# The end of a chunk in an output projection: stores in pieces, sums a row at a time, a gain vector loaded in quarters

## The chip, the cores and the metric

The kernel runs on one core of a Trainium2 chip. A core has five engines, each with an instruction stream of its own that it takes strictly in order: TensorE (PE; products and, listed apart as PEld, the loads of its weights), VectorE (DVE), ScalarE (ACT), GpSimd (POOL) and SyncE (SP). Transfers between HBM and the on-chip memory SBUF are issued by an engine's queue (SPq, ACTq, POOLq) and carried out by 16 shared DMA engines. Products go to PSUM, from where VectorE and ScalarE read them.

The metric is the device time of one execution, in microseconds; the median of several runs counts.

## The reference

One inference step of a one-layer encoder with two groups of heads, for 1024 prompt rows and 128 sample rows (8 streams of 16), all in float32. What matters here is its end:

```python
y = jnp.concatenate([y_sb, y_r], axis=-1)          # 2048 wide, from both groups of heads
out = jnp.einsum('bte,ed->btd', y, w_out)          # w_out: 2048 x 2048
x = x + rms_norm(out, norm_post)                   # rms over the 2048 columns of a row
```

So each of the 1152 rows of `out` needs its mean square over all 2048 columns before any of its columns can be finished: `x + out * norm_post / sqrt(mean(out^2) + eps)`.

## The kernel before

Rows are handled in tiles of 128: eight of the prompt (0 to 7) and SAMPLE. The input projection, both attentions and the retention fill the first 1980 us or so; they leave the concatenated heads, transposed, in HBM (`s_y`). The output projection then takes nine row tiles in three chunks of three: chunk 1 is (0, 1, 2), chunk 2 is (4, 5) and (6), chunk 3 is (3, SAMPLE) and (7).

**Panels.** A chunk is computed in panels of 512 columns (`out_panel`, L1010). For each of 16 blocks `k` of 128 inner rows, a 128 x 512 block of `w_out` is loaded by SP (L1018) and split into a high and a low half (`split`, L128): ScalarE writes the high half rounded to fp32r (L129), VectorE the rest (L130). Then each of the three row tiles takes three products (high x high, L1028; high x low weights, L1029; low x high, L1030), which add up in the row tile's own PSUM bank. The buffers `wr`, `wh` and `wl` of a block exist four times, so the splits can run some blocks ahead of the products. Panels use two PSUM pools by turns.

**Sums.** When a panel is through, `take` (L1074) is called for each row tile: ScalarE squares the bank and sums the squares along the row into one column of `ssq` (L1076), VectorE multiplies the bank by `norm_post` into the row's `out` buffer (L1077). `norm_post` lies in `gpost`, the same 2048 values on all 128 partitions, loaded by one transfer on ScalarE's queue (L1045). That buffer, like `rp` and the second PSUM pool, is opened only when the stage of the attentions has closed (L1040). Chunk 1's first panel is computed within that stage, among its last jobs (L1036).

**Finish.** After the fourth panel, `scales` (L1079) turns the four sums of squares into 1/rms (L137 to L143), and `store` (L1084) finishes the rows in halves of 1024 columns. For the first and second row tile VectorE scales and adds `x` in one instruction (L1090); for the third ScalarE scales (L1087) and GpSimd adds `x` (L1088). The transfer to HBM is issued from ScalarE's queue (L1091), behind its sum. The chunk's `x` rows were loaded in its third and fourth panels (`load_x_rows`, each tied behind a load of `w_out` in SP's queue, L1020). There are five `out` buffers for rows, three for `x` rows and two for `ssq`.

**Chunk 3** is different: its last panel is 256 columns wide, and the other 256 columns' weights are kept split in SBUF (`keep_last`), so that the rows end one after the other, each with its own scales and four pieces of 512 columns, stored from SP's queue (L1108 to L1120).

**Jobs and ticks.** Side work is written as generators. `Job(steps, after)` puts one into a list; `tick()` (L173), called once after each row tile's three products, advances a clock and runs the next step of at most one job that is due; a step's `yield` says how many ticks later the next one is due. `fetch` (L1004) loads and splits the next chunk's rows that way, a step every 6 ticks, during the first two panels of a chunk. `drain` ticks until a job is done.

The order in which the program writes instructions is a priority: a planner lays the streams out by its own estimate of when each instruction's inputs are there, so an instruction can stand ahead of others that were written before it. On the chip the streams are then taken in that order, and an engine waits for the inputs of its next instruction.

Of the kernel before, what the change touches and what calls it, by code (L numbers as in the profile page):

```python
# [16 lines left out]
P = 128  # L17
D = 2048
# [30 lines left out]
D_TI = (32, 13)  # L49
D_OUT = 4  # L50
D_KL = 29
D_MR = 6
EPS = 1e-6
SCALE = 1.0 / math.sqrt(P)
# [4 lines left out]
def tile_hybrid_step(  # L59
# [26 lines left out]
    nc = tc.nc  # L86
# [86 lines left out]
    def tick():  # L173
        clock[0] += 1
        for job in jobs:
            if job.at <= clock[0]:
                wait = step(job)
                jobs.remove(job)
                if wait is None:
                    job.done = True  # L180
                else:
                    job.at = clock[0] + wait
                    jobs.append(job)
                return

    def drain(job):
        while job is not None and not job.done:
            tick()
# [4 lines left out]
    def moving(pool, n):  # L193
        return [list(x) for x in zip(*(moving_part(pool, n, q) for q in range(KT // WQ)))]

    def load_moving(mov, at, n, src, stage=None):
        hi, lo = mov
        for k in range(KT):
# [7 lines left out]
            split(hi[q][:, j, at : at + n], lo[q][:, j, at : at + n], r)  # L206
            yield D_MR

# [91 lines left out]
    with ExitStack() as s1:  # L300
# [47 lines left out]
        with tc.tile_pool(name="p0", bufs=2) as p0, tc.tile_pool(name="p0s", bufs=1) as p0s, tc.tile_pool(  # L348
# [50 lines left out]
            scales = [stats(0)]  # L399
            for i, t in enumerate(tiles):  # L400
# [6 lines left out]
                if i == 1:  # L407
                    w4 = list(load_w(col(4, 0)))
                    loaded += [load_x(t) for t in tiles[3:]]
                    acc = acc_banks(g0)  # L410
# [482 lines left out]
        for gi, g in enumerate(GROUPS):  # L893
            tiles, n, nt = g["tiles"], g["n"], len(g["tiles"])
# [141 lines left out]
        panel0 = out_panel(chunk1, 0, (accp,), D_OUT, loads)  # L1036
# [3 lines left out]
    with ExitStack() as s3:  # L1040
        c3 = s3.enter_context(tc.tile_pool(name="c3", bufs=1))
        rp = s3.enter_context(tc.tile_pool(name="rp", bufs=1))
        accq = s3.enter_context(tc.tile_pool(name="accq", bufs=2, space=PSUM))
        gpost = c3.tile([P, D], F32, name="gpost")
        nc.scalar.dma_start(gpost, norm_post[0].partition_broadcast(P))  # L1045

        LAST = slice(7 * 256, 8 * 256)

        def keep_last(at):

            hi, lo = main
            for q in range(KT // WQ):
                for j in range(0, WQ, 2):
                    wr = wp.tile([P, 2, 256], F32, name="wr4", tag="wr")
                    k = (q * WQ + j) * P
                    nc.sync.dma_start(wr, w_out[0, k : k + 2 * P, LAST].rearrange("(k p) e -> p k e", p=P))
                    split(hi[q][:, j : j + 2, at : at + 256], lo[q][:, j : j + 2, at : at + 256], wr)
                    yield D_KL

        def out_project(chunk, panel0=None, kept=None):  # L1060
            m = len(chunk)
            parts = 4 if kept is None else 5
            outs = [rp.tile([P, D], F32, name="out", tag="out", bufs=5) for _ in chunk]
            ssq = rp.tile([P, m, 5], F32, name="ssq3", tag="ssq3", bufs=2)
            xrs = []

            def load_x_rows():
                for t, _, _, _ in chunk:
                    xr = rp.tile([P, D], F32, name="xr", tag="xr", bufs=3)
                    nc.sync.dma_start(xr, x_rows(t))  # L1070
                    xrs.append(xr)
                    yield

            def take(n, a, c, cols):  # L1074
                sq = rp.tile([P, 512], F32, name="sq3", tag="sq3", bufs=1)
                nc.scalar.activation(sq[:, : a.shape[1]], a, AF.Square, accum_out=ssq[:, n, c : c + 1])  # L1076
                nc.vector.tensor_tensor(outs[n][:, cols], a, gpost[:, cols], ALU.mult)  # L1077

            def scales(n0, n1):  # L1079
                tot = rp.tile([P, n1 - n0], F32, name="tot", tag="tot", bufs=2)  # L1080
                nc.vector.tensor_reduce(tot, ssq[:, n0:n1, :parts], mybir.AxisListType.X, ALU.add)
                return inv_rms(rp, tot, D, f"out{n1 - n0}")

            def store(n, rs, cols, pool, q=nc.scalar):  # L1084
                o = outs[n][:, cols]
                if pool:
                    nc.scalar.activation(o, o, AF.Copy, scale=rs)  # L1087
                    nc.gpsimd.tensor_tensor(o, o, xrs[n][:, cols], ALU.add)  # L1088
                else:
                    nc.vector.scalar_tensor_tensor(o, o, rs, xrs[n][:, cols], ALU.mult, ALU.add)  # L1090
                q.dma_start(y_rows(chunk[n][0])[:, cols], o)  # L1091

            rows = load_x_rows()
            for p in range(4):
                width = 512 if kept is None or p < 3 else 256
                acc = panel0
                if p or not panel0:
                    acc = out_panel(chunk, p, (accp, accq), 1, None, rows if p >= 2 else None, width)
                for n in range(m):
                    take(n, acc[n][:, :width], p, slice(p * 512, p * 512 + width))  # L1100
            if kept is None:
                rs = scales(0, m)
                for half in range(2):
                    for n in range(m):
                        store(n, rs[:, n : n + 1], slice(half * D // 2, (half + 1) * D // 2), n == m - 1)
                return
            drain(job)
            for n, (_, _, (hi, lo), at) in enumerate(chunk):  # L1108
                a = accp.tile([P, 512], F32, name="a4", tag=f"acc{n % 2}")[:, :256]
                ts = slice(at, at + P)  # L1110
                for k in range(KT):
                    q, j = divmod(k, WQ)
                    wh, wl = (main[c][q][:, j, kept : kept + 256] for c in range(2))
                    nc.tensor.matmul(a, hi[q][:, j, ts], wh, start=(k == 0), stop=False)
                    nc.tensor.matmul(a, hi[q][:, j, ts], wl, start=False, stop=False)
                    nc.tensor.matmul(a, lo[q][:, j, ts], wh, start=False, stop=(k == KT - 1))
                take(n, a, 4, LAST)
                rs = scales(n, n + 1)
                for c in (3, 0, 1, 2):
                    store(n, rs, slice(c * 512, (c + 1) * 512), c == 3, nc.sync)  # L1120

        side = moving(c3, P)
        chunk2 = part(1, (4, 5), main, 3 * P), part(1, (6,), side, 0)
        chunk3 = part(0, (3, SAMPLE), main, 0), part(1, (7,), main, 2 * P)
        ready = [Job(fetch(c), 4) for c in chunk2]
        out_project(chunk1, panel0)
        for job in ready:
            drain(job)
        ready = [Job(fetch(c), 4) for c in chunk3]
        out_project(chunk2[0] + chunk2[1])  # L1130
        for job in ready:
            drain(job)
        keep = 3 * P
        job = Job(keep_last(keep), D_KL)
        out_project(chunk3[0] + chunk3[1], kept=keep)


# [70 lines left out]
```

## Time and profile before

| | |
|---|---|
| runs | 2405.13, 2405.88, 2412.4 us |
| median | 2405.88 us |
| profiled execution, first to last instruction (the page has no other time of it) | 2398.4 us |
| TensorE busy | 2331.4 us, 97% |
| VectorE, ScalarE, GpSimd busy | 52%, 38%, 27% |
| mean granted TensorE clock | 0.994 |
| products of the output projection's panels (L1028 to L1030) | first at 1981.7 us, last started at about 2371 us |

How to read the rows: in a timeline, start in us, duration in us, engine (with q: its queue), line, operation, what is written `<-` what is read, partitions x elements, count, and in brackets how long the engine had been idle before and what ended that. Several like instructions in a row are merged into one with their count. In groups: count, busy time, mean ns of one, idle time before. In windows: stretch, length, then busy time and count of each engine named, granted clock, share of the DMA engines, GB/s.

### The profile page before, as it was taken

Reading aid. Unit: us, or ns where it says so; the run is one execution under the profiler, and the core shown is the slowest. Engines: PE = TensorE matmul, PEld = TensorE weight load, DVE = VectorE, ACT = ScalarE, POOL = GpSimd, SP = SyncE. Lnnn points to the kernel's source line nnn. Section 1 sums busy time; section 2 is a strip of 40 time slices with the busy share of each in tenths; the row PEclk is TensorE's granted clock in tenths of the full one; section 3 lists DMA queues with packets and bytes.
Section 4 is the critical chain, followed back from the end, with each engine's and each line's share of the span. In section 5 each row is a group of like instructions: output and inputs, shape, how many; then the busy total and the mean of one; then the engine's idle time right before and its main releaser. Section 6 shows DMA issues by size and latency. Waiting matters only on the chain.

```text
span 2398.4 us, 40493 instructions
## 1 busy us (share of the span) xinstructions
PE 2331.4 (97%) x14832; PEld 2093.7 (87%) x14832; DVE 1257.5 (52%) x2434; ACT 919.6 (38%) x1933; POOL 643.0 (27%) x1029
## 2 busy tenths in 40 slices
PE   7999999999999999998999999999999999999998
PEld 7998899999999999988878889889898887878787
DVE  7245545445554555445545554554554665564544
ACT  6323333333333333324433434343343454543343
POOL 3144353444344353443202112020221230000000
PEclk9999999999999999999999999999999999999999
DMA  7658879797889879798975565565565666765554
GB/s 244 164 131 209 162 169 196 169 203 166 184 179 194 184 167 194 176 198 198 200 191 151 139 157 149 133 157 146 142 160 139 157 177 181 231 207 176 191 182 132
DMA packets 674890, 418.68 MB, mean 175 GB/s; under 512 B 224513, under 2 KB 619777, under 8 KB 672257
## 3 DMA queue, kind: packets, MB, share of 16 engines
q1 hardware_dynamic: 524272, 285.99, 47.8%
q0 software_dynamic: 32256, 71.36, 13.6%
q10 hardware_dynamic: 118160, 58.74, 9.1%
q8 instruction: 116, 1.90, 0.4%
q14 instruction: 86, 0.70, 0.1%
HBM read 336.24 MB, written 79.69 MB: 173 GB/s over the span
## 4 chain that ended last, share of the span: by engine, by line
PE 87%; DVE 4%; DMA 4%; issue 2%; ACT 1%; POOL 1%; ACTq 0%; DVEq 0%; SPq 0%; POOLq 0%
PE acc L227 45%; PE accn L286 17%; PE a L1029 5%; PE a L1030 5%; PE a L1028 5%; PE pa L616 3%; PE z L586 2%; DMA wr<-w_in 1%; PE zc L659 1%; PE pd L726 1%; DMA mr<-s_h 1%; DVE wl L130 1%; PE pa L770 1%; DVE out L1090 1%; PE rs L752 1%
## 5 line engine op out<-in xcount | busy, mean ns | idle before, releaser
L227 PE MATMUL acc<-mh,wh 128*128 128x256 f32 (+2 forms) x2304 | 664.3, 341 | 6.4 <-ACT wh L129 6.0
L227 PE MATMUL acc<-ml,wh 128*128 128x384 f32 (+2 forms) x2304 | 663.0, 340 | 0.0
L130 DVE TENSOR_TENSOR wl<-wr,wh 128x512 fp32r<-128x512 f32 (+1 forms) x576 | 392.7, 688 | 515.5 <-ACT wh L129 508.3
L227 PE MATMUL acc<-mh,wl 128*128 128x256 f32 (+2 forms) x2304 | 658.9, 339 | 0.6 <-DVE wl L130 0.5
L129 ACT ACTIVATE wh<-wr 128x512 fp32r<-128x512 f32 (+1 forms) x576 | 356.9, 624 | 713.1 <-PE acc L227 243.4
L227 PEld LDWEIGHTS acc<-mh,wh 128*128 128x128 f32 x2304 | 420.2, 189 | 43.3 <-ACT wh L129 7.1
L227 PEld LDWEIGHTS acc<-mh,wl 128*128 128x128 f32 x2304 | 424.4, 189 | 31.4 <-issue 2.1
L227 PEld LDWEIGHTS acc<-ml,wh 128*128 128x128 f32 x2304 | 422.6, 189 | 33.2 <-issue 5.3
L643 POOL DMA_DIRECT2D kc<-cache_sb_k x512 | 332.4, 655 | 369.8 <-DVE kcT L681 207.5
L286 PE MATMUL accn<-whn,mh 128*128 128x256 f32 x1152 | 329.0, 287 | 0.9 <-ACT whn L129 0.8
L286 PE MATMUL accn<-wln,mh 128*128 128x256 f32 x1152 | 326.2, 283 | 0.7 <-DVE wln L130 0.7
L286 PE MATMUL accn<-whn,ml 128*128 128x256 f32 x1152 | 326.0, 283 | 0.0
L286 PEld LDWEIGHTS accn<-whn,mh 128*128 128x128 f32 x1152 | 220.5, 192 | 10.8 <-issue 6.7
L1029 PE MATMUL a<-wl,mh 128*128 128x512 f32 (+1 forms) x576 | 219.7, 381 | 7.8 <-DVE wl L130 7.8
L286 PEld LDWEIGHTS accn<-wln,mh 128*128 128x128 f32 x1152 | 221.2, 192 | 1.7 <-DVE wln L130 0.9
L286 PEld LDWEIGHTS accn<-whn,ml 128*128 128x128 f32 x1152 | 221.2, 192 | 0.0
L1030 PE MATMUL a<-wh,ml 128*128 128x512 f32 (+1 forms) x576 | 218.9, 380 | 0.0
L1028 PE MATMUL a<-wh,mh 128*128 128x512 f32 (+1 forms) x576 | 218.0, 380 | 0.0
L130 DVE TENSOR_TENSOR wln<-wrn,whn 128x512 fp32r<-128x512 f32 x128 | 87.5, 687 | 119.2 <-ACT whn L129 118.5
L129 ACT ACTIVATE whn<-wrn 128x512 fp32r<-128x512 f32 x128 | 80.1, 633 | 152.2 <-PE accn L286 69.8
L1029 PEld LDWEIGHTS a<-wl,mh 128*128 128x128 f32 x576 | 108.3, 188 | 30.5 <-DVE wl L130 9.9
L479 POOL DMA_DIRECT2D be<-s_be x128 | 94.2, 742 | 132.7 <-DMA s_be<-be 114.7
(189 smaller groups left out, 2604.8 us busy)
## 6 DMA issues: line engine op xcount, KB each, us to landing
wr<-w_in SPq DMA_DIRECT2D x384, 256.0 KB, 4.2
wr<-w_out SPq DMA_DIRECT2D x184, 256.0 KB, 3.6
wrn<-w_in SPq DMA_DIRECT2D x128, 256.0 KB, 3.1
kc<-cache_sb_k POOLq DMA_DIRECT2D x512, 64.0 KB, 4.5
vc<-cache_sb_v SPq DMA_DIRECT2D x64, 512.0 KB, 8.6
xt<-x_prompt SPq DMA_DIRECT2D x8, 1024.0 KB, 5.6
xr<-x_prompt SPq DMA_DIRECT2D x8, 1024.0 KB, 6.2
out<-out ACTq DMA_DIRECT2D x12, 512.0 KB, 2.9
```

The costliest lines, as they stand in the source:

```text
L129: nc.scalar.activation(hi, src, AF.Copy)
L130: nc.vector.tensor_tensor(lo, src, hi.bitcast(F32), ALU.subtract)
L227: last = nc.tensor.matmul(a[:, :m], lhs[:, j, :], rhs[w][:, j, o : o + m], start=(w == 0 and j == 0 and n == 0), stop=(w == KT // WQ - 1 a ...
L286: anchor[0] = nc.tensor.matmul(a, lhs[q][:, jj, ts], rhs[:, j, :], start=(w == 0 and j == 0 and n == 0 and t % 2 == 0), stop=(w == KT // 2 ...
L479: q.dma_start(raw[32 * i : 32 * i + 32, :].rearrange("p (k a) -> p k a", a=32), s[:, :, 32 * i : 32 * i + 32].rearrange("k (j b) a -> b (k ...
L586: nc.tensor.matmul(z[:, :c], q2[a][:, i * P : (i + 1) * P], k2[b][:, s : s + c], start=(m == 0), stop=(m == 2),)
L616: nc.tensor.matmul(po[:, :P], at[:, j, :], vn[:, j, :], start=(j == 0), stop=(j == t))
L643: nc.gpsimd.dma_start(kc[32 * i : 32 * i + 32, :].rearrange("p (k d) -> p k d", d=32), cache_k[0, 2 * c + j, s * 512 : (s + 1) * 512, h, 3 ...
L659: mm = nc.tensor.matmul(z[r, :], qp[:, j, r], ready[2 * j + c // 2][:, c % 2, :], start=(j == 0), stop=(j == 1),)
L1028: nc.tensor.matmul(a[:, :width], hi[q][:, j, ts], wh, start=(k == 0), stop=False)
L1029: nc.tensor.matmul(a[:, :width], hi[q][:, j, ts], wl, start=False, stop=False)
L1030: nc.tensor.matmul(a[:, :width], lo[q][:, j, ts], wh, start=False, stop=(k == KT - 1))
```

## The change

`norm_post` is loaded by four transfers of 512 columns instead of one of 2048. In chunks 1 and 2 the panel sums become jobs: the three calls of `take` come 4 ticks after the panel (12 for chunk 1's first) and 4 ticks apart, within the next panel. The fourth panel's job goes on, also a step every 4 ticks, with the scales and then twelve stores of 512 columns instead of six of 1024: four column pieces by three row tiles. It runs along the products of the next chunk. Chunk 3 takes its sums as before, and drains the earlier chunks' jobs after its panels.

```diff
+D_TK = 4
+D_FIN = 4
...
-        nc.scalar.dma_start(gpost, norm_post[0].partition_broadcast(P))
+        for c in range(4):
+            nc.scalar.dma_start(
+                gpost[:, c * 512 : (c + 1) * 512], norm_post[0, c * 512 : (c + 1) * 512].partition_broadcast(P)
+            )
...
-                for n in range(m):
-                    take(n, acc[n][:, :width], p, slice(p * 512, p * 512 + width))
+
+                def take_rows(acc=acc, p=p, width=width):
+                    for n in range(m):
+                        take(n, acc[n][:, :width], p, slice(p * 512, p * 512 + width))
+                        yield D_TK
+
+                def finish_rows():
+                    yield from take_rows()
+                    rs = scales(0, m)
+                    yield D_FIN
+                    for c in range(4):
+                        for n in range(m):
+                            store(n, rs[:, n : n + 1], slice(c * 512, (c + 1) * 512), n == m - 1)
+                            yield D_FIN
+
+                if kept is not None:
+                    for _ in take_rows():
+                        pass
+                elif p < 3:
+                    Job(take_rows(), D_TK if p or not panel0 else 3 * D_TK)
+                else:
+                    rows_done.append(Job(finish_rows(), D_TK))
             if kept is None:
-                rs = scales(0, m)
-                for half in range(2):
-                    for n in range(m):
-                        store(n, rs[:, n : n + 1], slice(half * D // 2, (half + 1) * D // 2), n == m - 1)
                 return
+            for done in rows_done:
+                drain(done)
             drain(job)
...
+        rows_done = []
```

## The prediction

> **What bounds the kernel now.** I read the page first, busy times and then the chain that ended last.
>
> ```profile
> span 2398.4 us, 40493 instructions
> ...
> PE 2331.4 (97%) x14832; PEld 2093.7 (87%) x14832; DVE 1257.5 (52%) x2434; ACT 919.6 (38%) x1933; POOL 643.0 (27%) x1029
> ...
> PE 87%; DVE 4%; DMA 4%; issue 2%; ACT 1%; POOL 1%; ACTq 0%; DVEq 0%; SPq 0%; POOLq 0%
> ```
>
> TensorE sets the time nearly everywhere. The change cannot shorten a product, so it is worth only what TensorE loses around the lines that it touches. Next I asked for TensorE's waits over the whole output projection (1975 to 2398 us), and there is one row:
>
> ```profile
> PE a L1029 <- DVE wl L130: 7.8, 5, 2.3
> ```
>
> Five waits, all for a weight's low half. What they cost is read from the rate. I cut the stage into stretches of 48 products of line 1029 each (a panel is 16 k by 3 rows):
>
> ```profile
> 2018.02:2053.28 35.26, 18.79 (x48) 9.01 (x49) 1.00 0.63 190
> 2053.28:2085.92 32.64, 18.67 (x48) 9.01 (x49) 1.00 0.76 238
> 2085.92:2118.56 32.64, 18.67 (x48) 9.01 (x49) 1.00 0.66 208
> 2118.56:2154.59 36.03, 18.91 (x48) 9.01 (x49) 1.00 0.74 228
> ...
> 2219.86:2252.50 32.64, 18.67 (x48) 9.01 (x49) 1.00 0.49 160
> 2252.50:2288.54 36.04, 18.93 (x48) 9.01 (x49) 1.00 0.64 212
> 2288.54:2321.18 32.64, 18.67 (x48) 9.01 (x49) 1.00 0.48 147
> ```
>
> The columns are stretch, its length, TensorE busy and count, weight loads, granted clock, DMA share, GB/s. A clean panel takes 32.64 us at clock 1.00, so 0.68 us per row's three products (one tick) and 2.04 us per k. Three panels are long: chunk 1's panel 1 by 2.62, the first panel of chunk 2 by 3.39, the first of chunk 3 by 3.40. Sum 9.41 us. The "7.8" above is smaller because the last product before a wait still counts as busy while it drains and the restart is slow.
>
> The other panel ends (2086, 2187, 2220, 2321) lose nothing, though each has its three squares and gains in one go: taking panel sums a row at a time has nothing to win there.
>
> The long first panels come from VectorE and ScalarE at the end of a chunk:
>
> ```profile
> 2121.29 0.69 DVE L130 TENSOR_TENSOR wl<-wr,wh 128x512 fp32r<-128x512 f32 x1
> ...
> 2122.89 7.02 DVE L1090 SCALAR_TENSOR_TENSOR out<-out,out3r,xr 128x1024 f32<-128x1024 f32 x4
> 2129.83 0.68 DVE L130 TENSOR_TENSOR wl<-wr,wh 128x512 fp32r<-128x512 f32 x1
> 2132.03 3.67 DVE L130 TENSOR_TENSOR wl<-wr,wh 128x512 fp32r<-128x512 f32 x3 [1.52 <-ACT wh L129]
> 2122.66 0.63 ACT L129 ACTIVATE wh<-wr 128x512 fp32r<-128x512 f32 x1 [1.31 <-PE a L1030]
> ...
> 2124.21 6.07 ACTq L1091 DMA_DIRECT2D out<-out  x5
> 2130.33 1.15 ACT L1087 ACTIVATE out<-out,out3r 128x1024 f32<-128x1024 f32 x1 [5.99 <-DVE out L1090]
> 2124.42 3.21 POOL L1088 TENSOR_TENSOR out<-out,xr 128x1024 f32<-128x1024 f32 x1 [141.37 <-DMA wr<-w_out]
> 2131.56 2.40 POOL L1088 TENSOR_TENSOR out<-out,xr 128x1024 f32<-128x1024 f32 x1 [3.92 <-ACT out L1087]
> 2128.58 0.39 PE L1028 MATMUL a<-wh,mh 128*128 128x512 f32 x1
> 2130.57 0.50 PE L1029 MATMUL a<-wl,mh 128*128 128x512 f32 x1 [1.60 <-DVE wl L130]
> ```
>
> VectorE runs its four scale-and-add instructions without a break for 7 us. ScalarE's queue holds the five store issues, each behind its sum, so the next high half comes only after 2130.33. The high half of 2122.66 was ready at 2123.29 and its low half could have been at 2123.98; TensorE, at its own pace, asked for it at 2128.58 + 0.23 = 2128.81. So the splits run 4.83 us ahead of TensorE: whatever delays a split by less costs nothing. Here it came 6.5 us late, at 2130.51 (TensorE restarts at 2130.57), and a second split is caught by the second GpSimd sum (2132.03: three splits in 3.67 us instead of some 2.0).
>
> Chunk 1's panel 1 is another case, the load of norm_post:
>
> ```profile
> 2020.21 0.34 ACTq L1045 DMA_DIRECT2D gpost<-norm_post  x1
> ...
> 2028.40 1.89 DVE L1077 TENSOR_TENSOR out<-a,gpost 128x512 f32<-128x512 f32 x3 [5.15 <-DMA gpost<-norm_post]
> 2030.21 0.68 DVE L130 TENSOR_TENSOR wl<-wr,wh 128x512 fp32r<-128x512 f32 x1
> DMA to landing us min/median/max: 8.1/8.1/8.1
> ```
>
> VectorE waits 5.15 us in order, does three products of 0.63, and only then the split that TensorE needs.
>
> **The change, part by part.** (1) *norm_post in quarters, and panel 0's sums 12 ticks later.* ScalarE issues four loads instead of one, 3 x 0.34 = 1.0 us more of its queue, under the 4.83. I leave the first issue at 2020.2, since its buffer lies in the space of the stage that closes there. The first quarter's landing is bounded by the 256 KB weight loads from below and by the whole load from above:
>
> ```profile
> wr<-w_out SPq DMA_DIRECT2D x184, 256.0 KB, 3.6
> ...
> out<-out SPq DMA_DIRECT2D x12, 256.0 KB, 2.6
> ```
>
> So it lands between 2020.2 + 3.6 = 2023.8 and 2020.2 + 8.1 = 2028.3. I take 2024 to 2025, since a quarter is the same 256 KB over 128 partitions as the row of 3.6. The 12 ticks (8.2 us of products) move the sums behind four k of splits in the program, but the order on an engine isn't the program's, as these rows show:
>
> ```profile
> 2021.26 0.60 ACT L1076 ACTIVATE sq<-a 128x512 f32<-128x512 f32 x1 [0.50 <-DMA wr<-w_out]
> ...
> 2021.85 0.30 ACT L129 ACTIVATE mh<-mr 128x128 fp32r<-128x128 f32 x1
> 2022.05 0.59 ACT L1076 ACTIVATE sq<-a 128x512 f32<-128x512 f32 x1
> ```
>
> A split of the fetch, written after all three squares, stands between the first two: the planner fills a free engine with what it holds ready. So I assume that the sum may still stand as early as before (about 2023.2) and wait one to two us: nothing is lost within 4.83. Gain 2.62; if the quarter lands like the whole, 0 to 1.3, because two of the three products (2 x 0.63) may no longer stand ahead of the split.
>
> (2) *The finish in twelve pieces per chunk.* Its last sums, the scales and then a piece every 4 ticks: 3 x 4 + 4 + 12 x 4 = 64 ticks, 43.5 us, across panel 0 and into panel 1 of the next chunk. Removed: both blocks of 7 us. Added, by rows of the tail, which stores in such pieces already:
>
> ```profile
> L1090 DVE SCALAR_TENSOR_TENSOR out<-out,out1r,xr x9: 742/751/1787, 2379.4 to 2392.3; 128x512 f32<-128x512 f32 x9
> L1090 DVE SCALAR_TENSOR_TENSOR out<-out,out3r,xr x8: 1271/1284/3429, 2122.9 to 2262.6; 128x1024 f32<-128x1024 f32 x8
> L1088 POOL TENSOR_TENSOR out<-out,xr 128x512 f32<-128x512 f32 x3 | 5.2, 1739 | 120.3 <-ACT out L1087 116.2 <-DMA out<-out 4.1
> L1087 ACT ACTIVATE out<-out,out1r x3: 721/723/727, 2379.4 to 2390.9; 128x512 f32<-128x512 f32 x3
> ```
>
> Per chunk: VectorE 8 x 0.75 = 6.0 us (before 4 x 1.28 = 5.1); GpSimd 4 x 1.74 = 7.0; ScalarE 4 x 0.72 = 2.9 and 12 issues x 0.34 = 4.1 (before 6). A piece beside a GpSimd sum takes up to 1.79 instead of 0.75, so each GpSimd sum costs VectorE 1.04 more, 4.2 a chunk. Room per 2.04 us of a k, from
>
> ```profile
> 2142.00:2182.00 40.00, 40.00 (x178) 33.14 (x177) 20.12 (x38) 17.66 (x40) 0.00 (x0) 1.00 0.59 172
> ```
>
> (after the length: TensorE, weight loads, VectorE 20.12, ScalarE 17.66, GpSimd none; splits, fetches and one panel's sums are in it): some 20 us are free on either in 40 us, and 43.5 us of ticks ask for 10.2 + 1.9 (last sums) on VectorE and 7.0 + 1.8 on ScalarE; GpSimd has nothing else here. It fits even when the planner packs the pieces into the gaps of 8 k: per k 20.12 x 2.04 / 40 = 1.03, one piece 0.75 and half a GpSimd hold 0.52 make 2.30, 0.26 over, 2.1 in all, under 4.83. So both first panels go back to 32.64: gain 3.39 + 3.40.
>
> (3) *Waits that move.* Each store still waits on ScalarE for its sum; queued behind it are the next high halves, and behind those TensorE. One wait is now at most one piece or one GpSimd sum (1.79). Chunk 2's third row uses the buffer of chunk 1's first row (five buffers), whose last piece is due at tick 56 and lands some 2.6 us (4 ticks) later; the sum that needs it is due at tick 60. VectorE may wait one or two us there, with the next split behind it: hidden by 4.83, less if a piece is late too. SP's loads of x rows come from panel 2 on, 96 ticks in, behind the finish. The final panel and tail keep their order.
>
> Sum, from the profiled span: 2398.4 - 2.62 - 3.39 - 3.40 = 2389.0. The median of the runs lies 7.5 us above that span, so 2396.5; I add 0.3 for waits that just come through: **2396.8 us**.
>
> A rule that speaks against the change: the Trainium skill, SBUF — State Buffer, "Who interferes with whom", has a VectorE instruction with two SBUF inputs fully blocked while a GpSimd instruction that reads SBUF holds the shared pair. The 3.43 us piece beside the 3.21 us GpSimd sum agrees; by that rule the eight GpSimd sums hold VectorE up to 1.74 each, 14 us in all, and if none of that were covered the sum would be 2411.
>
> **The rivals.** *ScalarE fills up with waiting stores.* A round of 12 ticks is 8.16 us. ScalarE's work in it in chunk 2: 17.66 x 8.16 / 40 = 3.6, one scale 0.72, three issues x 0.34, sum 5.3. If two issues wait 1.79 and one 1.74, it is 10.6: over by 2.5 a round, 10 in four rounds, less 4.83, some 5 us lost; in chunk 3, with four high halves of 0.63 and no fetches, 9.6, over by 1.4, in all 0.8. That gives 2403 at most; it begins at (8.16 - 5.3 + 4.83 / 4) / 3 = 1.4 us of wait per issue, and halfway it gives **2400**. For it: the 5.99 us wait above. Against: that one stood behind four long sums, a piece is 0.75.
>
> *The first stall stays* (the change doesn't do what it says there): the quarter lands at 8.1 or the sums wait for all four. 2396.8 + 2.6 = **2399.4**. For it: the order may leave the sum at 2023. Against: at the kernel's start norm_pre comes in two halves, and the first is used at 7.95, where the second, issued 0.42 later and landing in 6.5 to 7.2, is in at 1.7 + 6.5 = 8.2 at the earliest.
>
> ```profile
> L380 SPq DMA_DIRECT2D gpre<-norm_pre x2: 421/422/423, 1.3 to 1.7; - x2
> ...
> DMA to landing us min/median/max: 6.5/6.9/7.2
> ```
> ```profile
> 7.95 0.43 DVE L392 TENSOR_TENSOR xt<-xt,gpre 128x256 f32<-128x256 f32 x1
> ```
>
>
> *The pieces bunch, and GpSimd blocks VectorE.* No piece depends on another, so the planner may put a row of pieces ahead of the splits. Then a boundary has 8 x 0.75 + 4 x 1.74 = 13.0 us of VectorE in place of 7.0, 6.0 more behind the same cover: +12 for both, -2.6 for the first stall, 2405.9 + 9.4 = **2415**. It decides once VectorE runs over 4.83 us without a split. For it: the burst at 2122.89. Against: there the pieces stand before the splits in the program, now most stand behind.
>
> **How the numbers follow.** Forecast 0.58, ScalarE 0.17, first stall 0.13, bunching 0.12. A measurement of this kernel tells about 0.3% (7.2 us) from no change: faster is below 2398.7, the forecast alone; 2399.4 and 2400 are the same, with 0.30; slower 0.12. The range starts at 2395, 2396.5 with no leftover less the 0.75 by which the lowest run lies under the median and another 0.75 for stalls elsewhere in the stage; it ends at 2405, past the first two rivals, and leaves out the bunching. The forecast's own range is 2395 to 2398.7.
>
> **What would show it.** Right: stretches of 48 products in the first panels of chunks 2 and 3 and in chunk 1's panel 1 at 32.6 to 33; no TensorE wait for a low half between 2018 and 2354; pieces on VectorE with splits in between; the product with gpost waiting under 3 us. Wrong: ScalarE idle for sums of line 1090 or 1088 in a row (first rival); 35 us left in chunk 1's panel 1 (second); a VectorE run of pieces over 5 us (third); or lost time in a panel that is clean now.

## The result, and the profile after

| | before | changed |
|---|---|---|
| median of 9 runs each | 2405.33 us | 2396.79 us |
| lowest to highest | 2401.15 to 2412.4 us | 2393.76 to 2401.33 us |
| time of the changed kernel over that of before | | 0.9969, 95% interval 0.996 to 0.9978 |
| profiled execution, first to last instruction | 2398.4 us | 2396.1 us |

The medians differ by 8.5 us, the two profiled spans by 2.3. The panels tell why. Below is the same view as for before, stretches of 48 products of one line (L1031 now; the change moves the lines of the projection by two or more). The columns are stretch, its length, TensorE busy and count, weight loads, granted clock, DMA share, GB/s.

```profile
2024.39:2057.03 32.64, 18.69 (x48) 9.02 (x49) 1.00 0.67 204
...
2122.31:2154.95 32.64, 18.69 (x48) 9.01 (x49) 1.00 0.78 243
2154.95:2188.29 33.34, 18.93 (x48) 9.01 (x49) 1.00 0.52 160
...
2253.57:2286.21 32.64, 18.69 (x48) 9.02 (x49) 1.00 0.72 235
```

Chunk 1's panel 1 (first row), and the first panels of chunks 2 and 3 (second and fourth row), took 35.26, 36.03 and 36.04 us before; all three are clean now. One panel that was clean, chunk 2's second, is 0.70 too long. So the projection gained 9.41 - 0.70 = 8.71 us, close to the difference of the medians, 8.54. The span shows less because this execution came to chunk 1's panel 1 later, at 2024.4 instead of 2018.0 us, 6.4 us behind, through waits in the earlier stages, which the change doesn't touch. One stretch holds most of it. TensorE's busy time there, first before and then changed (then clock, DMA share, GB/s):

```profile
1000.00:1200.00 200.00, 191.19 (x1262) 0.98 0.92 203
```
```profile
1000.00:1200.00 200.00, 186.07 (x1217) 0.97 0.88 199
```

Runs of one and the same kernel wander by as much: 2399.5 to 2410.17 us in 31 runs of the kernel before. For a change of 9 us in one stage the lengths of that stage's panels are the finer measure, and the experiments below are read by them first.

TensorE's waits from 1975 to 2398 us in the changed kernel (engine, operation, what it waited for: us in total, times, longest). The five waits for a low half, 7.8 us, are one of 0.2 now; the other two rows lie in the attentions' last jobs.

```profile
PE pa L772 <- DVE so L621: 1.1, 1, 1.1
PE pS L787 <- DVE rkn L855: 0.7, 1, 0.7
PE a L1031 <- DVE wl L132: 0.2, 1, 0.2
```

The end of chunk 1 in the changed kernel, by the timelines of VectorE, GpSimd and ScalarE:

```profile
2126.64 0.75 DVE L1095 SCALAR_TENSOR_TENSOR out<-out,out3r,xr 128x512 f32<-128x512 f32 x1
2127.31 0.68 DVE L132 TENSOR_TENSOR wl<-wr,wh 128x512 fp32r<-128x512 f32 x1
2127.91 3.76 DVE L1095 SCALAR_TENSOR_TENSOR out<-out,out3r,xr 128x512 f32<-128x512 f32 x4
2131.60 0.68 DVE L132 TENSOR_TENSOR wl<-wr,wh 128x512 fp32r<-128x512 f32 x1
2132.20 1.41 DVE L1095 SCALAR_TENSOR_TENSOR out<-out,out3r,xr 128x512 f32<-128x512 f32 x2
...
2134.13 0.74 DVE L1095 SCALAR_TENSOR_TENSOR out<-out,out3r,xr 128x512 f32<-128x512 f32 x1
...
2134.41 3.35 POOL L1093 TENSOR_TENSOR out<-out,xr 128x512 f32<-128x512 f32 x1 [5.27 <-ACT out L1092]
...
2134.63 0.63 ACT L131 ACTIVATE wh<-wr 128x512 fp32r<-128x512 f32 x1 [0.30 <-PE a L1032]
2137.79 2.19 ACTq L1096 DMA_DIRECT2D out<-out  x2
2140.08 0.63 ACT L131 ACTIVATE wh<-wr 128x512 fp32r<-128x512 f32 x1 [4.82 <-DMA out<-out]
...
2148.33 0.34 ACTq L1096 DMA_DIRECT2D out<-out  x1
```

The planner does not keep the 64 ticks (43.5 us) that the program asks for: VectorE's eight pieces stand within 8.2 us (2126.64 to 2134.87) and the last store goes out at 2148.33, some 22 us after the first piece. But splits stand between the pieces, and the longest run without one is 3.76 us, under the lead of 4.83. What is new is on ScalarE: its next high half starts at 2140.08, after 4.82 us without work, because two stores stand ahead of it, one of them behind a GpSimd sum of 3.35 us.

The loads of norm_post in the changed kernel:

```profile
2026.58 1.97 ACTq L1048 DMA_DIRECT2D gpost<-norm_post  x4
2030.61 0.69 DVE L1082 TENSOR_TENSOR out<-a,gpost 128x512 f32<-128x512 f32 x1 [1.18 <-DMA gpost<-norm_post]
2031.21 0.68 DVE L132 TENSOR_TENSOR wl<-wr,wh 128x512 fp32r<-128x512 f32 x1
```

The first quarter is there 4.0 us after its issue, VectorE waits 1.18 us for it instead of 5.15, and a split follows the first product instead of all three.

### The profile page after: what moved, and what is told of

The parts are those of the page before. It is cut to its first block, busy times and chain, and to the rows that moved or that the text cites. A ratio compares the mean times of both kernels' runs of the same rounds, so it can differ in the third digit from the quotient of the medians.

```text
span 2396.1 us, 40529 instructions
## 1 busy us (share of the span) xinstructions
PE 2332.6 (97%) x14832; PEld 2094.6 (87%) x14832; DVE 1254.6 (52%) x2442; ACT 919.6 (38%) x1937; POOL 646.2 (27%) x1033
## 4 chain that ended last, share of the span: by engine, by line
PE 83%; DMA 7%; DVE 4%; issue 2%; ACT 2%; SPq 1%; POOL 0%; DVEq 0%; ACTq 0%; POOLq 0%
PE acc L229 44%; PE accn L288 17%; DMA mr<-s_y 4%; PE a L1031 3%; PE a L1032 3%; PE a L1030 3%; PE pa L618 3%; PE z L588 2%; DMA wr<-w_in 2%; PE zc L661 1%; PE pd L728 1%; DMA mr<-s_h 1%; DVE wl L132 1%; DVE ml L132 1%; ACT mh L131 1%
## 5 line engine op out<-in xcount | busy, mean ns | idle before, releaser
L1031 PE MATMUL a<-wl,mh 128*128 128x512 f32 (+1 forms) x576 | 219.5, 381 | 0.2 <-DVE wl L132 0.2
L1031 PEld LDWEIGHTS a<-wl,mh 128*128 128x128 f32 x576 | 108.4, 188 | 21.2 <-DVE wl L132 0.9
```

The lines of the kernel that those rows point to most:

```text
L1031: nc.tensor.matmul(a[:, :width], hi[q][:, j, ts], wl, start=False, stop=False)
```

## The experiments

Each time stands against the kernel before on the same chip. "Too long" sums up what the nine panels from chunk 1's panel 1 to chunk 3's third exceed 32.64 us by (before: 9.41).

| kernel | panels too long, us | median, us | median of before | ratio, 95% interval |
|---|---|---|---|---|
| changed | 0.70 | 2396.79 | 2405.33 | 0.9969, 0.996 to 0.9978 |
| quarters alone | 6.93 | 2403.78 | 2404.77 | 1.0003, 0.999 to 1.0015 |
| finish in pieces alone | 1.31 | 2399.49 | 2404.77 | 0.9977, 0.9966 to 0.9987 |
| delay of panel 0's sums alone | 6.80 | 2404.44 | 2404.77 | 0.9997, 0.9983 to 1.001 |
| pieces in a burst | 14.85 | 2408.9 | 2404.77 | 1.0021, 1.0008 to 1.0034 |
| changed, again | 0.37 | 2397.68 | 2404.54 | 0.997, 0.9958 to 0.9982 |
| no GpSimd | 0.00 | 2395.43 | 2404.54 | 0.9963, 0.995 to 0.9976 |
| halves in a job | 0.70 | 2395.34 | 2404.54 | 0.9963, 0.9948 to 0.9978 |
| before, 3 more buffers at the end of SBUF | 4.12 | 2399.53 | 2404.54 | 0.9981, 0.9971 to 0.9992 |
| before, 3 more buffers beside the others | 7.66 | 2403.62 | 2405.53 | 0.9993, 0.9983 to 1.0003 |
| burst, 3 more buffers beside the others | 7.05 | 2402.47 | 2405.53 | 0.9987, 0.9974 to 1.0001 |
| stores from GpSimd's queue | 5.81 | 2400.23 | 2405.53 | 0.9979, 0.9967 to 0.9992 |
| stores from SP's queue | 4.31 | 2398.67 | 2405.53 | 0.9975, 0.9963 to 0.9987 |

The panels come from one profiled execution each, so a few tenths of a microsecond there are no verdict.

**Quarters alone.** The kernel before with this hunk only:

```diff
-        nc.scalar.dma_start(gpost, norm_post[0].partition_broadcast(P))
+        for c in range(4):
+            nc.scalar.dma_start(
+                gpost[:, c * 512 : (c + 1) * 512], norm_post[0, c * 512 : (c + 1) * 512].partition_broadcast(P)
+            )
```

> The kernel before with norm_post in quarters and nothing else. Theory: chunk 1's panel 1 was long because VectorE waited 5.15 us for the whole load and then did three products ahead of the split; the first quarter lands some 4 us after its issue, so three products still ahead of that split end about 6.5 us after the issue instead of 10, inside the 4.83 us by which splits run ahead: 48 products of line 1029 in 32.64 us there (before 35.26), the first panels of chunks 2 and 3 stay at 36.03, time 2.6 us below the kernel before. Rival: the quarter alone does nothing (it lands with the others, or only the later place of the sums helps): 34 to 35.3 us, time unchanged.

Chunk 1's panel 1 took 32.81 us instead of 35.26, so 2.45 of the 2.62 come from the quarters, set against the one profiled execution of before; the chunk ends stayed at 36.01 and 36.03. VectorE waited 3.9 us here too, since the first quarter came only 4.9 us after its issue, but that is still 3.2 us earlier than the whole load of before. The whole time does not resolve so little.

**Finish in pieces alone.** Sums at once and one load, as before; only the scales and the stores become a job:

```diff
+            def finish_rows():
                 rs = scales(0, m)
-                for half in range(2):
+                yield D_FIN
+                for c in range(4):
                     for n in range(m):
-                        store(n, rs[:, n : n + 1], slice(half * D // 2, (half + 1) * D // 2), n == m - 1)
+                        store(n, rs[:, n : n + 1], slice(c * 512, (c + 1) * 512), n == m - 1)
+                        yield D_FIN
+
+            if kept is None:
+                rows_done.append(Job(finish_rows(), D_FIN))
```

> The kernel before with only the finish of chunks 1 and 2 as a job of twelve pieces, a step every 4 ticks; panel sums in one go, norm_post in one load. Theory: the first panels of chunks 2 and 3 fall from 36.03 to 32.64 us each, up to 0.7 more in chunk 2 as in the changed kernel; chunk 1's panel 1 stays at 35.26; time 6.1 to 6.8 us below before. Rival: sums taken a row at a time are needed as well: over 34 us in a first panel, time less than 4 us below.

Both chunk ends were clean at 32.64, without a rest anywhere near them. Chunk 1's panel 1 stayed too long, by 1.31 only: the single load landed in 6.8 us here, not 8.1, and VectorE waited 3.88 for it instead of 5.15. The finish is the part that carries the gain.

**Delay alone.** The kernel before, with chunk 1's first panel summed 12 ticks later and 4 ticks apart:

```diff
+                if p == 0 and panel0:
+                    def first_rows(acc=acc):
+                        for n in range(m):
+                            take(n, acc[n], 0, slice(0, 512))
+                            yield 4
+                    Job(first_rows(), 12)
```

> The kernel before with only panel 0's sums as a job 12 ticks later, a row every 4 ticks; norm_post in one load. Theory: one more split gets ahead of the waiting product, so the late split is the next one, which TensorE wants 2.04 us later, and two products of 0.63 stand ahead of it instead of three: the 2.62 us fall to 0 to 0.3, chunk 1's panel 1 at 32.6 to 33.0 us, time 2.3 to 2.6 us below before. Rival: only the quarters matter: 35.3 us, time unchanged.

Chunk 1's panel 1 was 32.64, with the whole norm_post in one load that landed in 7.2 us. VectorE still waited 4.0 us for it, but with one more split ahead. So the delay is as good as the quarters, and the changed kernel has both where either does it. Panel sums a row at a time in the other panels moved nothing in any run.

**The burst.** The changed kernel, with the fourth panel's job run out at once where it was made a job:

```diff
-                    rows_done.append(Job(finish_rows(), D_TK))
+                    for _ in finish_rows():
+                        pass
```

> The changed kernel with the twelve pieces written all at once at the end of their chunk, ahead of the next splits, instead of as a job. Theory: what counts is how long VectorE and ScalarE run without a split. Eight pieces and four GpSimd sums make a run of 10.2 to 13.0 us on VectorE, against 7.0 in the kernel before, so the first panels of chunks 2 and 3 take 39 to 42 us each and the time is 4 to 10 us above the kernel before, 2409 to 2415. Rival: the smaller pieces are what helped: first panels at 32.6 to 34 us, 2397 us.

From the same view of panels (columns as above), and from VectorE's timeline:

```profile
2123.69:2162.96 39.27, 19.93 (x48) 9.50 (x49) 0.91 0.72 218
2260.88:2301.74 40.86, 20.52 (x48) 9.86 (x49) 0.87 0.61 187
```
```profile
2128.02 7.50 DVE L1095 SCALAR_TENSOR_TENSOR out<-out,out3r,xr 128x512 f32<-128x512 f32 x8
2135.45 0.68 DVE L132 TENSOR_TENSOR wl<-wr,wh 128x512 fp32r<-128x512 f32 x1
2139.47 3.25 DVE L132 TENSOR_TENSOR wl<-wr,wh 128x512 fp32r<-128x512 f32 x4 [3.35 <-ACT wh L131]
```

Eight pieces in a row hold VectorE 7.5 us, the next high halves come late from ScalarE as well (the last bracket), and the first panels are 3 to 5 us longer than with the long finish. Small pieces are worth nothing by themselves; what counts is where they stand. Part of the excess is the clock of 0.91 and 0.87 (last section): behind the last pause of each panel products still start every 0.43 us instead of 0.23 for a while, by their starts some 1.6 and 2.6 us in all, an estimate.

**The changed kernel again, and three variants of its finish.** The first run is the same kernel. In the second, VectorE finishes the third row too, so that GpSimd and ScalarE's scaling are out of it:

```diff
-                            store(n, rs[:, n : n + 1], slice(c * 512, (c + 1) * 512), n == m - 1)
+                            store(n, rs[:, n : n + 1], slice(c * 512, (c + 1) * 512), False)
```

In the third the job stores six halves of 1024, a step every 8 ticks:

```diff
-                    for c in range(4):
+                    for half in range(2):
                         for n in range(m):
-                            store(n, rs[:, n : n + 1], slice(c * 512, (c + 1) * 512), n == m - 1)
-                            yield D_FIN
+                            store(n, rs[:, n : n + 1], slice(half * D // 2, (half + 1) * D // 2), n == m - 1)
+                            yield 2 * D_FIN
```

> The changed kernel once more, without an edit. It lost 0.70 us in chunk 2's panel 1 (33.34 us), after ScalarE had stood 4.82 us at two store issues behind a GpSimd sum of 3.35 us. Theory: that delay is about as long as the splits' lead of 4.83 us, so the loss comes and goes with the length of that one sum: 32.64 to 34 us there, all other panels 32.64. Rival: the loss belongs to the order of the streams and returns at 33.3 us.

> The changed kernel with the third row's pieces in chunks 1 and 2 on VectorE too (12 scale-and-adds of 0.75 us), none on ScalarE and GpSimd. Theory: GpSimd's sums and VectorE's sums hold each other up, and ScalarE's issues wait for both; without GpSimd no piece takes over 0.8 us, ScalarE waits under 2 us at an issue, and all panels take 32.64 us; time 0 to 0.7 us below the changed kernel. Rival: VectorE now has 9 us of pieces per chunk instead of 6 and is what runs late: 33 to 36 us in the first panels of chunks 2 and 3.

> The changed kernel with six stores of 1024 columns per chunk, as before, but still as a job, a step every 8 ticks. Theory: the place in the order counts, not the size; the planner lets splits in between, so no run without a split is longer than two sums and a GpSimd hold, 2 x 1.28 + 2.15 = 4.7 us, just under 4.83: first panels of chunks 2 and 3 at 32.6 to 33.5 us, time within 1 us of the changed kernel. Rival: halves are too long: 35 us or more in a first panel.

Again, the changed kernel lost a little in chunk 2, now 0.34 us in its first panel and 0.03 in its second; neither the theory nor the rival had it in the first. Here the rest can be followed instruction by instruction, through GpSimd, ScalarE, VectorE and TensorE:

```profile
2147.63 1.29 POOL L1093 TENSOR_TENSOR out<-out,xr 128x512 f32<-128x512 f32 x1 [4.64 <-ACT out L1092]
...
2148.95 0.34 ACTq L1096 DMA_DIRECT2D out<-out  x1
2149.41 0.63 ACT L131 ACTIVATE wh<-wr 128x512 fp32r<-128x512 f32 x1 [1.86 <-DMA mr<-s_y]
...
2150.07 0.69 DVE L132 TENSOR_TENSOR wl<-wr,wh 128x512 fp32r<-128x512 f32 x1 [2.41 <-ACT wh L131]
...
2150.41 0.39 PE L1030 MATMUL a<-wh,mh 128*128 128x512 f32 x1
2150.82 0.50 PE L1031 MATMUL a<-wl,mh 128*128 128x512 f32 x1
```

GpSimd's last sum ends at 2147.63 + 1.29 = 2148.92; its store follows at 2148.95; the high half queued behind it starts at 2149.41, the low half ends at 2150.76, and TensorE takes it at 2150.82, 0.41 after the product before it instead of 0.23. The releaser in the bracket, a load, is not what came last: the row above it is.

Without GpSimd every panel was 32.64 (to 0.01), and VectorE's longest run of pieces was four in 2.73 us. Halves in a job had clean chunk ends but for 0.70 in chunk 2's first panel, with one run of two halves of 4.62 us. So it is the spreading that counts, not the size of a piece. By whole times the three cannot be told apart: 2397.68, 2395.43 and 2395.34, with intervals that overlap.

**More lead instead of less work.** If a chunk's end costs only what the splits are late by, more buffers for split weights should hide even the old finish. The kernel before, with every fifth to seventh block of seven in a pool of its own:

```diff
+                weights = more if more and turns[0] % 7 >= 4 else wp
+                turns[0] += 1
-                wr = wp.tile([P, width], F32, name="wr3", tag="wr")
+                wr = weights.tile([P, width], F32, name="wr3", tag="wr")
...
+        wq = s3.enter_context(tc.tile_pool(name="wq", bufs=3))
```

First the pool was opened last in the projection's stage:

> The kernel before, with seven buffers for a block's weights and their halves instead of four from chunk 1's panel 1 on, nothing moved. Theory: each buffer adds a k of 2.04 us to the 4.83 us by which splits run ahead, 10.95 in all; the three delays of before (6.5 us at a chunk's end, some 7.4 at norm_post) lie below that, so all panels take 32.64 us and the time falls by about 9.4 us, as much as by the change. Rival: the lead is not set by these buffers, and the panels stay at 35 to 36 us.

TensorE waited for nothing from 2018 to 2370 us, with the old finish in place, and no panel stands out. But from chunk 1's panel 1 on every full panel took 33.04 to 33.16 us. TensorE's timeline in a panel of that kernel:

```profile
2060.40 0.39 PE L1032 MATMUL a<-wh,mh 128*128 128x512 f32 x1
...
2061.10 0.40 PE L1032 MATMUL a<-wh,mh 128*128 128x512 f32 x1
...
2063.86 0.39 PE L1032 MATMUL a<-wh,mh 128*128 128x512 f32 x1
...
2064.54 0.39 PE L1032 MATMUL a<-wh,mh 128*128 128x512 f32 x1
```

A row's three products take 0.70 us in some blocks (2060.40 to 2061.10) and 0.68 in others (2063.86 to 2064.54), in a pattern that repeats with the seven buffers. So the pool was opened first instead, which puts its buffers beside the other four:

> The kernel before (long finish, one load of norm_post) with three more weight buffers, like the last experiment with them, but the pool with the three is opened first after the attentions' stage closes, so that it lies next to the other four and not at the end of SBUF. Theory: what made all panels 33.05 to 33.16 us there is where the added buffers lie, not their number; then the panels of chunks 2 and 3 are 32.64 again, with no TensorE wait at the chunk ends, and the whole is some 9.4 us under the kernel before, about 2395. Rival: more buffers, or two pools taken by turns, cost the 0.02 us per row themselves; then the panels stay at 33.1 and the whole at about 2399.5.

The two panels that matter, columns as above:

```profile
2023.08:2062.98 39.90, 19.32 (x48) 9.37 (x49) 0.96 0.70 226
2128.26:2160.90 32.64, 18.67 (x48) 9.01 (x49) 1.00 0.74 248
```

The theory was right in its point: panels are 32.64 again, chunk 2's first among them, and chunk 3's first is 0.40 over. Its sum was wrong: chunk 1's panel 1 rose to 39.90. TensorE waits there once, and SP's queue shows where it began (2014 to 2030 us):

```profile
PE a L1032 <- ACT wh L129: 5.3, 1, 5.3
```
```profile
SPq L1022 <- DMA s_y<-sg: 2.2, 1, 2.2
```

SP's load of a block waits for a store of the attentions (`s_y <- sg`), and three block loads then go out within a microsecond from 2025.0 on, beside the 1 MB of norm_post; blocks landed up to 8.2 us after their issue. That the new buffers reuse the memory which that store still read fits the row and the place of the pool; it was not tried by itself.

The burst with these buffers:

> The burst kernel (twelve pieces written at once at the chunk's end; its first panels took 39.27 and 40.86 us, 6.6 and 8.2 too long) with the same three more weight buffers next to the other four. Theory: a chunk's end costs what the splits are late by, less their lead over TensorE; three blocks more of lead are 3 x 2.04 = 6.12 us, so the first panels come to about 33.2 and 34.7 us, 2398 in all. Rival: the burst holds an engine for good (work, not lateness), and first panels stay at 39 or more, 2405 to 2409.

First panels came from 39.27 and 40.86 down to 32.64 and 33.88 us, by 6.63 and 6.98 for a lead of 6.12 (a little more, since the half clock went too): a chunk's end is a matter of lateness, and the rival of lost work falls. The whole was 2402.47, not 2398, mainly because chunk 1's panel 1 was 38.45 here too.

**Who waits at the store.** The changed kernel, with the pieces' stores on another queue:

```diff
-                            store(n, rs[:, n : n + 1], slice(c * 512, (c + 1) * 512), n == m - 1)
+                            store(n, rs[:, n : n + 1], slice(c * 512, (c + 1) * 512), n == m - 1, nc.gpsimd)
```

and the same with `nc.sync`.

> The changed kernel with the pieces' stores issued from GpSimd's queue, so that ScalarE no longer waits at an issue. Theory: the 0.37 to 0.70 us that the changed kernel still loses in a first panel of chunk 2 come from ScalarE's queue standing at issues behind late sums; then all panels are 32.64 us and the whole is 0.4 to 0.7 us under the changed kernel, 2395.5 to 2397. Rival: the loss comes from GpSimd's long sums holding VectorE's splits, or from the fetches; then 0.4 to 0.7 us stay in that panel.

> The changed kernel with the pieces' stores issued from SP's queue, which brings the weight blocks. Theory: a store waits for its sum in order, so the next weight load waits with it; loads run well ahead, so the first panels of chunks 2 and 3 are 32.64 to 34 us, with ScalarE waiting for loads of wr in place of sums. Rival: the loads are so far ahead that nothing of it reaches TensorE: 32.64 everywhere, as the changed kernel without its last 0.4 to 0.7 us.

Neither theory nor rival held for GpSimd's queue: chunk 2's and 3's first panels took 35.94 and 35.15. ScalarE's timeline there:

```profile
2144.61 0.72 ACT L131 ACTIVATE mh<-mr 128x256 fp32r<-128x256 f32 x2 [6.33 <-DMA mr<-s_y]
...
2278.29 1.26 ACT L131 ACTIVATE wh<-wr 128x512 fp32r<-128x512 f32 x2 [4.09 <-DMA wr<-w_out]
```

In chunk 2 ScalarE has no store to wait at any more, but a split of the next chunk's rows stands ahead of the weights' high halves, and its load is late: in this stretch (2122 to 2152 us) such loads landed after 1.9 to 6.7 us, against 2.5 to 4.7 in the second run of the changed kernel. Without the waits at stores the planner's order lets the twelve stores go out between 2127.4 and 2141.7, and all 16 DMA engines together were 92% busy from 2132 to 2142 (77% in that run of the changed kernel). That the loads are late because of these stores fits, and was not separated from the GpSimd issues of 0.55 us each; the kernel without GpSimd had up to 100% (2126 to 2136 us), and lost nothing. Chunk 3 fetches no rows; there ScalarE waited for a block of `w_out` itself (second row).

With SP's queue the first panels came out at 34.46 and 34.17, a little over what the theory had, and the second ones at 33.30 and 32.94. But its mechanism was not the main one. VectorE, GpSimd and ScalarE at the end of chunk 1, and what SP's block loads waited for (2119 to 2150 us):

```profile
2124.86 5.20 DVE L1095 SCALAR_TENSOR_TENSOR out<-out,out3r,xr 128x512 f32<-128x512 f32 x3
2129.98 1.78 DVE L132 TENSOR_TENSOR wl<-wr,wh 128x512 fp32r<-128x512 f32 x1
...
2124.69 6.53 POOL L1093 TENSOR_TENSOR out<-out,xr 128x512 f32<-128x512 f32 x4 [136.87 <-ACT out L1092]
...
2140.83 0.62 ACT L131 ACTIVATE mh<-mr 128x256 fp32r<-128x256 f32 x2 [5.00 <-DMA mr<-s_y]
```
```profile
SPq L1020 <- DVE wl L132: 7.7, 6, 4.2
...
SPq L1096 <- DVE out L1095: 2.6, 2, 1.4
```

ScalarE, which no longer stands at stores, scales the third row's four pieces by 2127.5; so GpSimd adds them one right after the other, and VectorE is held for three pieces and a split in a row, 6.9 us without a finished split. SP waits at stores 2.6 us in all, and 4.2 at once for that late split to free a buffer. Of the 1.83 us that chunk 2's first panel lost, some 0.4 lie right behind this hold (at 2131.81); most of the rest comes at 2142 and 2151, after ScalarE awaited loads of fetched rows for 5.00 and 3.67 us. In the changed kernel stores and splits stand between the four scalings on ScalarE and keep GpSimd's sums apart; how much of that is the waits at the stores, and how much the planner's order, was not separated.

## Why the prediction came out right, and where it did not

- **What bounds the kernel.** TensorE, and the three long panels alone: all three went to 32.64, by 2.62, 3.39 and 3.40 as the sum had it. 2396.8 was forecast and 2396.79 measured, but it is the panels that show the sum right (9.41 less 0.3 forecast, 9.41 less 0.70 and 0.37 measured). The median that the forecast starts from, 2405.88 of three runs, is 2405.33 with nine, and other groups of runs have medians of 2404.54 to 2405.53 before and 2397.68 after, so an agreement to 0.01 us is luck. Nor are the 7.5 us from the span to the median a fixed term: for the changed kernel they are 0.7 (2396.1 to 2396.79). Adding them works because the sum is then the median of before less 9.41.
- **Part (1), the gain vector.** The size was right (2.45 of 2.62 by the quarters alone, one execution) and so was the landing: 4.0 us after issue for the first, 3.9 to 5.9 for all four, between the two bounds. The product waited 1.18 us, inside "one to two". Left unsaid was that either half of the part is enough. The first stall is also no constant: the single load landed in 6.8, 7.2 and 8.1 us in three executions, and the panel lost 1.31 us for it with 6.8 and 2.62 with 8.1.
- **Part (2), the pieces.** Right that both first panels go back to 32.64, and for the reason given as a reserve: that it fits "even when the planner packs the pieces". It did pack them. A piece every 4 ticks over 43.5 us did not happen; 8.2 us on VectorE did, with a longest run of 3.76 against the lead of 4.83. The reserve's own sum, 2.1 us of the lead used, was near: the low half that VectorE finished at 2132.28 was taken by TensorE at 2134.60, so 2.32 us were left. The term that was mis-sized is the hold by GpSimd, 1.04 us a sum for VectorE, 4.2 a chunk. These rows of the changed kernel give the sixteen pieces of both chunks and the GpSimd sums of the projection, chunk 3's among them:

```profile
L1093 POOL TENSOR_TENSOR out<-out,xr 128x512 f32<-128x512 f32 x11 | 19.0, 1730 | 380.5 <-ACT out L1092 269.8 <-DMA wr<-w_out 110.7
L1095 DVE SCALAR_TENSOR_TENSOR out<-out,out3r,xr 128x512 f32<-128x512 f32 x16 | 13.3, 872 | 0.1
```

  A piece took 0.872 on average instead of 0.745: 16 x 0.127 = 2.0 us, 1.0 a chunk. The Trainium skill, SBUF — State Buffer, "Who interferes with whom", has the one that issues second blocked; the prediction took VectorE for that one throughout. The trace has both: four pieces in 3.76 instead of 3.0 beside one sum, and then a GpSimd sum of 3.35 us, where 1.29 is its time alone, beside VectorE's unbroken work. That moves the cost from VectorE to the store behind the sum.
- **Part (3), the waits that move.** This is the step that failed. It took one wait for "at most one piece or one GpSimd sum (1.79)", and set each wait alone against the whole lead. One wait was 4.82 us, made of the held sum (2134.41 to 2137.76) and two issues of 2.19 together. Yet it lost nothing there: chunk 2's first panel was 32.64. What it took was lead, and the lead did not come back. From the end of a low half to the start of its product there were 4.79 us at the end of chunk 1, 1.04 behind the long wait (product at 2144.80) and 0.77 at 2150.92; 4.79 were reached again only at 2176.10. Then something small comes through, in the changed kernel's first execution like this:

```profile
2155.46 0.62 ACT L131 ACTIVATE mh<-mr 128x256 fp32r<-128x256 f32 x2 [4.04 <-DMA mr<-s_y]
...
2156.64 1.29 DVE L132 TENSOR_TENSOR wl<-wr,wh 128x512 fp32r<-128x512 f32 x2
...
2157.38 0.50 PE L1031 MATMUL a<-wl,mh 128*128 128x512 f32 x1 [0.17 <-DVE wl L132]
```

  ScalarE awaits a load of the next chunk's rows for 4.04 us, the weights' splits stand behind it, and TensorE waits: the larger part of the 0.70 us in chunk 2's second panel. Why that load came 4.8 us after its issue was not shown. In the repeated run it was the wait of 1.86 us at the last store (the rows in the experiments), which cost 0.34 us, while 3.64 us at the place of the long wait cost nothing. So the first rival's mechanism, waits that add up, was there, but it cost 0.34 us where it can be followed and 0.70 at most, not the 3 or so of its 2400; the 0.3 "for waits that just come through" was the right term with too little in it. Chunk 3 has the same finish and lost nothing: its lead never fell below 2.2 us (1.8 in the repeated run). It fetches no rows, and that this is the difference fits, but was not tried by itself.
- **The rivals.** "The first stall stays" did not come about. "The pieces bunch" was only not the planner's choice: written in one go, the same pieces cost 3.24 and 4.82 us more than the long finish, 8.1 for both where 12 were forecast (and some 4.2 of the 8.1 are the half clock), and 2408.9 where 2415 was. Its threshold, VectorE over 4.83 us without a split, separates most runs with four buffers: runs of pieces of 2.73, 3.76 and 4.62 us went with 0 to 0.70 us lost in chunk 2, 5.20 (stores on SP's queue) with 1.8 in its first panel, 7.0 with 3.4, 7.5 with 6.6. It isn't the only way to lose the lead: with stores on GpSimd's queue runs of 3.58 and 4.79 us went with 3.3 and 2.5, by ScalarE's late loads.
- **Sums a row at a time** were worth nothing, as the clean panel ends said.

## What to carry to other kernels

Read first how far the feeding engines run ahead of the bound one, in microseconds. A run of side work below that lead costs nothing by itself, a longer one costs at least the excess. But the lead is a reserve that one delay after another uses up, and it has to be refilled in between: do not set each wait against the whole of it. Side work must be cut where it can be interleaved; cutting it without moving it made it worse here. A store's wait belongs to the queue it is issued from, so look at what stands behind it there before a queue is chosen; here ScalarE's lost least of three, and taking GpSimd out of the finish left no loss in any panel of the one execution profiled. For changes of a few tenths of a percent, measure the stage's own stretches, since runs wander by more than the change.

## What the runs showed of the hardware

- **A stall can cost the clock too.** In the burst kernel TensorE stood from its product at 2133.71 to 2136.18, and some 1.3 us after the restart the granted clock fell. Stretches of 2 us, TensorE busy and count, clock, DMA share, GB/s:

```profile
2134.00:2136.00 2.00, 0.10 (x1) 1.00 0.81 231
2136.00:2138.00 2.00, 1.82 (x7) 0.86 1.11 303
2138.00:2140.00 2.00, 1.41 (x4) 0.50 0.84 223
...
2144.00:2146.00 2.00, 2.00 (x9) 0.93 0.86 316
```

  Products came every 0.43 us instead of 0.23 from 2137.8 to 2144.4 us, less the two pauses in between. A pause of 2.43 us between starts in that kernel's chunk 3 and the 5.3 us wait of the kernel with three more buffers did the same (0.87 and 0.96 in the mean of the panel), while pauses of 2.67 us in the kernel before (at norm_post) and of 2.66 us with stores on GpSimd's queue left the clock at 1.00. The Trainium skill, TensorE: Matmul & The Clock Gate, "Part 1: The HAM clock gate (the "warmup" mystery)", has the array at half clock after an idle window of about 3.4 us that runs freely, with a start every 426.7 ns for 512 columns. The 0.43 us agrees. The pauses of 2.47 and 2.43 us are shorter than that window; why they sufficed, where 2.67 did not, is not settled by these runs.
- **Products on the buffers opened last were slower.** With three weight buffers in a pool opened last a row's three products took 0.70 us instead of 0.68, 3% more, in the three blocks of seven that use that pool (by their starts 2.09 to 2.10 us a block, the others 2.04 to 2.06); with the pool opened first no block shows it. The place is what was changed; the reason stays open.
- **A store's issue took 1.76 us** once on ScalarE's queue, where 0.34 is usual (the longest of the twelve stores of chunk 1). Its cause is open.
